# One list of weights for a two-layer trunk, and a freer order of its mixing stage, on one core

## The chip, the core and the metric

The kernel runs on one core of a Trainium2 chip. The core has five engines that run at the same time: TensorE (PE; its loads of the stationary operand are listed apart, as PEld), VectorE (DVE), ScalarE (ACT), GpSimd (POOL) and SyncE (SP), which here only starts transfers (DMA) between DRAM and the on-chip memory. Matmul results land in PSUM banks. Each engine works through its own instructions in order, and waits where an input is not there or a buffer is not free.

The metric is the device time of one launch in microseconds (us), the median over runs.

## The reference

A trunk of two layers on one sequence of 512 tokens with 1024 features, and 256 memory tokens. Each layer applies four steps, each behind an RMSNorm and added to the stream h:

```
h = h + 0.5 * (silu(u @ w_gate) * (u @ w_up)) @ w_out          # ffn1, 2816 wide
p = rmsnorm(h) @ w_mix_in                                       # 3712 columns
h = h + concat(short_conv(p_conv), hgrn2(p_hg), rwkv7(p_rw)) @ w_mix_out
h = h + softmax(q @ k_mem.T / 16) @ v_mem @ wo                  # 4 heads, k and v from rmsnorm(mem)
h = h + 0.5 * ffn2(rmsnorm(h))
```

`hgrn2` is a gated linear recurrence with 6 heads of 64; `rwkv7` is a recurrence with 6 heads of 64 whose state is updated for every token by a decay, a rank-one correction and a rank-one term. After both layers comes a last RMSNorm. All inputs and the output are fp32.

## The kernel before, in words

All activations lie as tiles of 128 features x 512 tokens in 69 slots of on-chip memory (names s_...). h itself is eight such tiles. A product of fp32 operands is made of three matmuls in a rounded format (fp32r): each operand is split into a high and a low part, and w·x, w·x_low and w_low·x are summed in PSUM (`mm3`). A product with 1024 input features is thus 24 matmuls of 128 x 512.

**Weights.** `load_w` fetches one weight tile of 128 x 1024: SP starts the transfer into `wst` (2 buffers), ACT copies it to `whi` in fp32r (3 buffers), DVE subtracts the two into `wlo` (3 buffers). This is "the split" of a weight. In the two feed-forward stages `group` calls `load_w` where the product stands in the program. In the mixing and cross-attention stages the products are in a queue, `Fill`, and `Fill.load` calls `load_w` for the next three products of that queue (AHEAD = 3). The queue of a stage is empty before the stage begins, and the products of the mixing stage's output are added to it only once their inputs are there, so the look-ahead does not pass the border of a stage.

**Order.** PE keeps program order. While the program is written out, a planner (`Clock`) keeps an estimate of when each engine is free and each tile is written; DVE's and ACT's instructions are put in order of their planned start. In the mixing and cross-attention stages `Fill.run` picks, again and again, between the next step (three matmuls) of the queue and the next piece of one of several chains of work, written as generators. A generator says what it needs (`Need`: tiles, finished products, free slots, free PSUM banks); its piece is taken once the planned time of these, less an allowance `ahead`, plus MARGIN (0.4 us) lies before PE's planned time. Generators marked calm are held back while DVE has more than 5 us of planned work.

**The mixing stage** (`mix`) first stores h in DRAM. Its 29 input products run in the order: RWKV decay, three pairs (of heads) of RWKV k, r, v, three pairs of HGRN f, v, q, gate, the RWKV gate, and two blocks of the convolution (cz, cx, cb). Among them run, as generators:

- `rw_inputs`, three times: prepares an RWKV pair;
- `rw_solve`: inverts 96 triangular 32 x 32 systems on DVE, in 30 steps of a multiplication and an addition each (tile G); behind it `rw_chain`, the serial recurrence over the chunks, and `rw_post`;
- one generator for HGRN: the gates of pair 0, then pair 0 with the gates of pair 1 in its middle, then pair 1 with those of pair 2, then pair 2, then the eight products of the stage's output over y columns 5 to 8. It starts when RWKV's third pair is prepared (key in2). Pair 2's four tiles wait in DRAM until they are used;
- `normed`: the norm of the memory tokens for the cross-attention (four tiles: two scalings by `rmem` and a split each). It waits for the convolution product cb0 (key), and in its loop for 8 and 7 free slots.

Then come the keys and values from the memory tokens (16 weight tiles) and the output products over columns 0 to 5.

In the `kernel.py` of before, line L286 stands for every instruction of DVE, ACT, POOL and SP (a wrapper that records them), L341 for every matmul and L345 for every transpose. Instructions are told apart by tile names: pb, pm, pt are PSUM banks (3, 3 and 2 of them), s a slot, vec a table of per-feature constants.

## Time and profile before

| what | value |
|---|---|
| time, median of 3 runs | 2483.07 us (2482.79 to 2483.42) |
| time of the profiled execution | 2484.71 us |
| span in its profile | 2482.9 us |
| granted TensorE clock, mean | 0.985 |
| PE busy | 2410.2 us, 97% |
| DVE busy | 1383.0 us, 56% |
| ACT busy | 997.0 us, 40% |
| mean DMA rate | 98 GB/s |

The span is the profiled stretch of one execution; about 1.8 us lie outside it. "Busy" leaves out waiting. The two layers take about 1230 us each; in the first, ffn1 ends near 380 us, mixing near 760 us, cross-attention near 880 us. A row of the timeline gives start, duration, engine, operation, the tile written and those read, and in brackets the idle time of the engine just before the row and what ended it. A row of the windows gives a stretch of the span, for each engine its busy time and number of instructions, then the granted clock as a share of full speed, the share of the DMA engines in use, and GB/s.

### The profile page before, as it was taken

The page shows a single profiled execution, that of the slowest core. Times are in us where ns is not written, and L with a number is a line of the kernel's source. Part 1 is how long each engine was busy: PE and PEld are TensorE (multiplying, and loading weights), DVE is VectorE, ACT ScalarE, POOL GpSimd, SP SyncE. Part 2 cuts the span into 40 slices and gives each one's busy share as a digit, 9 for nine tenths or more (in the row PEclk, how much of TensorE's full clock was granted, in tenths as well). Part 3 has the DMA queues.
Part 4 walks back from the last instruction along what each step waited for, and adds up shares of the span by engine and source line. Part 5 has one row for each costly group of instructions (what it writes and reads, how often), then busy time and mean ns, then how long its engine had stood idle before and what let it go on. Part 6 is the DMA issues. An engine that isn't in the chain of part 4 may idle for free.

```text
span 2482.9 us, 33542 instructions
## 1 busy us (share of the span) xinstructions
PE 2410.2 (97%) x13812; PEld 1977.9 (80%) x13812; DVE 1383.0 (56%) x2172; ACT 997.0 (40%) x1426; POOL 15.7 (1%) x22
## 2 busy tenths in 40 slices
PE   7999999999999999999999999999999999999997
PEld 6878887787867878888888888877887687888886
DVE  5434456788766544344544444567886656444344
ACT  4323235675654432222332222366765534322233
POOL 0000000000000000000000000000000000000000
PEclk9999999999999999999999999999999999999998
DMA  4323333233422123232333232423243212232322
GB/s 155 96 85 96 98 112 109 75 119 119 130 84 72 64 92 96 94 101 93 95 100 96 95 99 94 136 83 101 100 124 109 83 57 85 86 101 94 102 92 86
DMA packets 92008, 242.61 MB, mean 98 GB/s; under 512 B 21840, under 2 KB 24528, under 8 KB 91856
## 3 DMA queue, kind: packets, MB, share of 16 engines
q1 hardware_dynamic: 88544, 234.36, 29.9%
q10 hardware_dynamic: 3312, 6.12, 0.7%
q8 instruction: 108, 1.77, 0.3%
q14 instruction: 44, 0.36, 0.0%
HBM read 228.39 MB, written 12.06 MB: 97 GB/s over the span
## 4 chain that ended last, share of the span: by engine, by line
PE 89%; DVE 5%; ACT 4%; issue 1%; DMA 0%; SPq 0%; POOLq 0%; DVEq 0%; ACTq 0%
PE pb L341 80%; PE pm L341 6%; DVE s L286 4%; ACT s L286 3%; PE pt L341 1%; ACT L286 1%; PE pm L345 1%; DVE wlo L286 1%; ACT whi L286 0%; PE pt L345 0%; DMA s<-xT 0%; DVE G L286 0%; SPq L286 0%; ACT UV L286 0%; POOLq L1654 0%
## 5 line engine op out<-in xcount | busy, mean ns | idle before, releaser
L341 PE MATMUL pb<-s,whi 128*128 128x512 f32 (+1 forms) x6160 | 1901.1, 391 | 13.8 <-ACT whi L286 10.7
L341 PEld LDWEIGHTS pb<-s,whi 128*128 128x128 f32 x6160 | 1153.6, 190 | 258.0 <-ACT whi L286 12.4
L341 PE MATMUL pb<-s,wlo 128*128 128x512 f32 (+1 forms) x3080 | 1196.1, 388 | 30.0 <-DVE wlo L286 30.0
L341 PEld LDWEIGHTS pb<-s,wlo 128*128 128x128 f32 x3080 | 584.6, 190 | 153.8 <-DVE wlo L286 35.4
L286 ACT ACTIVATE s<-s 128x512 f32<-128x512 f32 (+2 forms) x458 | 284.5, 630 | 836.8 <-DVE s L286 835.0
L286 ACT ACTIVATE whi<-wst 128x1024 fp32r<-128x1024 f32 (+5 forms) x445 | 424.2, 969 | 394.7 <-PE pb L341 135.2
L286 DVE TENSOR_TENSOR wlo<-wst,whi 128x1024 fp32r<-128x1024 f32 (+5 forms) x445 | 495.9, 1116 | 153.2 <-ACT whi L286 152.4
L286 DVE TENSOR_TENSOR s<-pb,s 128x512 f32<-128x512 f32 (+1 forms) x345 | 236.6, 689 | 413.5 <-PE pb L341 363.7
L286 DVE TENSOR_TENSOR s<-s,s 128x512 f32<-128x512 f32 (+3 forms) x526 | 318.0, 622 | 144.2 <-ACT s L286 136.0
L286 DVE SCALAR_TENSOR_TENSOR s<-pb,s 128x512 f32<-128x512 f32 x96 | 66.4, 692 | 237.4 <-PE pb L341 237.4
L286 ACT ACT_TABLE_LOAD x84 | 107.8, 1283 | 3.1 <-PEq L1647 1.7
L286 DVE SCALAR_TENSOR_TENSOR s<-s,vec,s 128x512 fp32r<-128x512 f32 (+2 forms) x100 | 74.6, 750 | 9.4 <-ACT s L286 9.0
L341 PE MATMUL pm<-s,s 64*64 64x64 f32 (+2 forms) x1104 | 67.2, 256 | 10.5 <-DVE s L286 10.5
L341 PEld LDWEIGHTS pm<-s,s 64*64 64x64 f32 (+2 forms) x1104 | 62.5, 166 | 17.3 <-DVE s L286 10.8
L286 ACT ACTIVATE s<-s,vec 128x512 fp32r<-128x512 f32 (+1 forms) x90 | 64.4, 719 | 3.3 <-DMA s<-xT 1.7
L286 ACT COPY s<-pm 64x256 f32<-64x256 f32 (+3 forms) x69 | 23.3, 358 | 76.9 <-PE pm L341 66.0
L341 PE MATMUL pb<-whi,s 128*128 128x512 f32 x128 | 47.2, 414 | 0.0
L341 PEld LDWEIGHTS pm<-s 64*64 64x64 f32 (+1 forms) x1152 | 33.9, 130 | 9.6 <-issue 6.9
L341 PE MATMUL pm<-s 64*64 64x32 f32 (+1 forms) x1152 | 37.7, 216 | 0.0
L286 ACT ACTIVATE s<-pb 128x512 fp32r<-128x512 f32 x32 | 18.8, 596 | 37.0 <-PE pb L341 36.8
L286 DVE TENSOR_TENSOR s<-s 128x256 f32<-128x256 f32 (+1 forms) x79 | 31.4, 436 | 0.1
L341 PEld LDWEIGHTS pb<-whi,s 128*128 128x128 f32 x128 | 24.0, 188 | 6.0
(106 smaller groups left out, 726.5 us busy)
## 6 DMA issues: line engine op xcount, KB each, us to landing
wst<-ffn_w_in SPq DMA_DIRECT2D x175, 512.0 KB, 3.5
wst<-w_mix_in SPq DMA_DIRECT2D x58, 512.0 KB, 3.5
wst<-ffn_w_out SPq DMA_DIRECT2D x64, 448.0 KB, 3.3
wst<-ffn_w_out SPq DMA_DIRECT2D x32, 512.0 KB, 3.5
wst<-xattn_wk SPq DMA_DIRECT2D x16, 512.0 KB, 3.7
wst<-xattn_wv SPq DMA_DIRECT2D x16, 512.0 KB, 3.6
wst<-xattn_wq SPq DMA_DIRECT2D x16, 512.0 KB, 3.5
wst<-xattn_wo SPq DMA_DIRECT2D x32, 256.0 KB, 2.6
```

The source lines that it names most:

```text
L286: ins = fn(*args, **kw)
L341: self.pin(nc.tensor.matmul(*args, **kw))
L345: self.pin(nc.tensor.transpose(*args, **kw))
```

## The change

1. **One list of weights** (`Weights`, object W). The plan of all weight tiles, in the order in which the products run, is written before anything else (`plan_ffn`, `plan_mix`, `plan_xa`). `take` hands out the first entry; before and after each product the next tiles of the list are loaded and split until three are ahead (two while a product is under way), across stages and for products that are not in the queue yet. `Fill.load` goes, and `group` in the feed-forward stages takes from the same list. The buffers stay 2, 3 and 3.
2. **HGRN pairs.** Three generators in place of one, each waiting for its own gate product and 11 slots (7 for pair 0), no longer for RWKV's third pair. The last to end queues the output products. Pair 1's four tiles go through DRAM as pair 2's did: 8 stores and 8 fetches of 256 KB more over both layers.
3. **Memory norm.** `normed` waits for the product hv2 (HGRN, pair 2) and 12 free slots instead of cb0, and for 6 and 5 free slots in place of 8 and 7 in its loop.
4. **Constants.** MARGIN 0.4 to 0.15 us; the allowance `ahead` of a step of `rw_solve` 4.0 to 8.0 us.

The number of matmuls stays. Loads of ACT's function tables in the program go from 84 to 74.

```diff
@@ -104,10 +104,9 @@
 NSLOT = 69
 AHEAD = 3
-MARGIN = 0.4
+MARGIN = 0.15
 CALM = 5.0
 SPARE = 3
-NEXTAT = 2
 INF = 1 << 40
@@ -470,6 +469,31 @@
             ve.tensor_tensor(lo[:, cs], st[:, cs], f32(hi[:, cs]), op=ALU.subtract)
         return hi, lo
+    class Weights:
+        def __init__(self):
+            self.plan = deque()
+        def add(self, src, cols=1024):
+            self.plan.append([src, cols, None])
+        def ahead(self, n):
+            for e in list(self.plan)[:n]:
+                if e[2] is None:
+                    e[2] = load_w(*e[:2])
+        def take(self, src, cols):
+            have, c, w = self.plan[0]
+            assert (have.name, have.offset, c) == (src.name, src.offset, cols)
+            if w is None:
+                self.ahead(1)
+            w = self.plan.popleft()[2]
+            self.ahead(AHEAD - 1)
+            return w
+    W = Weights()
     def mm3(ps, w, wl, x, xl, start, stop):
         te.matmul(ps, w, x, start=start, stop=False)
         te.matmul(ps, w, xl, start=False, stop=False)
@@ -482,9 +506,10 @@
             mm3(ps, w[0][:, k * P:(k + 1) * P], w[1][:, k * P:(k + 1) * P], xh, xl, k == 0, k == n - 1)
             yield
-    def group(ps, src, cols, xs, w=None):
-        for _ in group_steps(ps, w or load_w(src, cols), xs):
+    def group(ps, src, cols, xs):
+        for _ in group_steps(ps, W.take(src, cols), xs):
             pass
+        W.ahead(AHEAD)
     class Fill:
...
@@ -508,33 +533,27 @@
                 return group_steps(box[0], w, xs)
             self.add(key, src, cols, steps, lambda: post(box[0]), room=room, xs=xs)
-        def load(self, n):
-            for e in list(self.q)[:n]:
-                if e[5] is None and e[1] is not None:
-                    e[5] = load_w(e[1], e[2])
-
         def ready(self):
             if self.cur:
                 return clock.pe
             if not self.q:
                 return None
-            e = self.q[0]
-            if (e[6] and e[6] not in self.done) or len(sl.free) < e[7]:
+            after, room, xs = self.q[0][5:]
+            if (after and after not in self.done) or len(sl.free) < room:
                 return None
-            self.load(AHEAD)
-            return max([bigs.free_at()] + [clock.when(x) for x in e[5] or ()]
-                       + [clock.when(x) for y in e[8][:3] for x in y])
+            W.ahead(AHEAD)
+            return max([bigs.free_at()] + [clock.when(x) for y in [W.plan[0][2]] + list(xs[:3]) for x in y])
         def step(self):
             if self.cur is None:
-                self.load(AHEAD)
-                key, _, _, steps, post, w = self.q.popleft()[:6]
-                self.cur = (key, iter(steps(w) or ()), post)
+                key, src, cols, steps, post = self.q.popleft()[:5]
+                self.cur = (key, iter(steps(W.take(src, cols)) or ()), post)
             key, g, post = self.cur
             if next(g, self) is self:
                 self.cur = None
                 self.done.add(key)
+                W.ahead(AHEAD)
                 if post:
                     post()
...
@@ -706,7 +725,7 @@
                 if f in between:
                     between[f]()
                 pg = big()
-                group(pg, w_in[l, f], 1024, n.x, between.get("w") if f == 0 else None)
+                group(pg, w_in[l, f], 1024, n.x)
                 if f or "w" not in between:
                     n.begin()
                 pu = small() if first else big()
@@ -974,7 +993,7 @@
             ve.tensor_tensor(tv, Gv[:, 0:k, k:k + 1].to_broadcast([n, k, w]),
                              Bv[k // 16][:, k % 16:k % 16 + 1, k + 1:].to_broadcast([n, k, w]), op=ALU.mult)
             ve.tensor_tensor(Gv[:, 0:k, k + 1:], Gv[:, 0:k, k + 1:], tv, op=ALU.add)
-            yield Need(Gv[:, 0:k, k + 1:], ahead=4.0)
+            yield Need(Gv[:, 0:k, k + 1:], ahead=8.0)
         sl.put(tmp, *B)
         sp.dma_start(Td, G[0:n, :])
         F.done.add((l, "solved"))
@@ -1125,7 +1144,7 @@
         sl.put(gd)
     def hg_gates(l, st, p):
-        q, f, v, g = (fetch(f"{w}{p}") if p == 2 else st["X"][f"{w}{p}"] for w in ("hq", "hf", "hv", "hgate"))
+        q, f, v, g = (fetch(f"{w}{p}") if p else st["X"][f"{w}{p}"] for w in ("hq", "hf", "hv", "hgate"))
         lb = lbt[:, l, p:p + 1]
         x, m, e1, e2 = sl.get(), sl.get(), sl.get(), sl.get()
@@ -1164,19 +1183,9 @@
         se.activation(dec, b3[:, :, C - 1], AF.Exp)
         return q, k, v, g, b, kh, dec
-    def hg_pairs(l, st, ys):
-        gates = []
-
-        def gate(p):
-            yield Need(keys=[(l, f"hg{p}"), (l, "in2")], room=11 if p == 2 else 7)
-            gates.append((yield from hg_gates(l, st, p)))
-
-        yield from gate(0)
-        for p in range(3):
-            yield from hg_pair(l, p, gates[p], ys, gate)
-
-    def hg_pair(l, p, gates, ys, gate):
-        q, k, v, g, b, kh, dec = gates
+    def hg_pair(l, st, p, ys):
+        yield Need(keys=[(l, f"hg{p}")], room=11 if p else 7)
+        q, k, v, g, b, kh, dec = yield from hg_gates(l, st, p)
         def tok(x):
...
@@ -1325,7 +1332,7 @@
                 X[key] = evac(n, ps)
                 if fn:
                     fn(X[key])
-                if key in ("hq2", "hf2", "hv2", "hgate2"):
+                if key[0] == "h" and key[-1] != "0":
                     send(key, X[key])
             add(key, j, post)
...
@@ -1372,15 +1380,16 @@
                     nxt.chunk(d)
             F.product((l, f"o{c0}{d}"), a["w_mix_out"][l, d, :, c0 * P:c1 * P], (c1 - c0) * P, ys, post)
-        def hgrn():
-            yield from hg_pairs(l, st, yb)
-            for d in range(ND):
-                yield Need(room=3)
-                unpark(d)
-                out(d, 5, 8, yb)
+        def hgrn(p):
+            yield from hg_pair(l, st, p, yb)
+            if all(yb):
+                for d in range(ND):
+                    yield Need(room=3)
+                    unpark(d)
+                    out(d, 5, 8, yb)
         F.run(seq(rw_solve(l, st), rw_chain(l, st), rw_post(l, st, ya)), mem_normed(),
-              calm=[rw_inputs(l, n, st, p) for p in range(3)] + [hgrn()])
+              calm=[rw_inputs(l, n, st, p) for p in range(3)] + [hgrn(p) for p in range(3)])
         ya += yc
         for d in range(ND):
             out(d, 0, 5, ya, True)
@@ -1422,11 +1431,11 @@
         mn, mx = [], []
         def normed():
-            yield Need(keys=[(l, "cb0")])
+            yield Need(keys=[(l, "hv2")], room=12)
             for i in range(4):
-                yield Need(room=8)
+                yield Need(room=6)
                 m = load_mem(i)
-                yield Need(m, room=7)
+                yield Need(m, room=5)
                 for u in range(2):
                     x = m[:, u * MEM:(u + 1) * MEM]
                     ve.scalar_tensor_tensor(x, x, col(l, "mem_norm", 2 * i + u), rmem, op0=ALU.mult, op1=ALU.mult)
@@ -1575,13 +1584,47 @@
         return nxt
+    def plan_ffn(l, which):
+        w_in, w_out = a[f"ffn{which}_w_in"], a[f"ffn{which}_w_out"]
+        for f0, f1 in SLABS:
+            for f in range(f0, f1):
+                W.add(w_in[l, f])
+                W.add(w_in[l, NF + f])
+            for d in range(ND):
+                W.add(w_out[l, d, :, f0 * P:f1 * P], (f1 - f0) * P)
+    def plan_mix(l):
+        rw, hg = ([[b + i + p for i in o] for p in range(3)] for b, o in ((RW0, (3, 0, 6)), (HG0, (3, 6, 0, 9))))
+        order = [RW0 + 9] + rw[0] + rw[1] + rw[2] + hg[0] + hg[1] + hg[2] + [RW0 + 10]
+        for j in order + [i + j for i in range(2) for j in (2, 4, 0)]:
+            W.add(a["w_mix_in"][l, j])
+        for j in range(2 * XH):
+            W.add(a["xattn_wk"][l, j])
+        for e in range(2):
+            for kp in range(4):
+                W.add(a["xattn_wv"][l, e, kp])
+        for c0, c1 in ((5, 8), (0, 5)):
+            for d in range(ND):
+                W.add(a["w_mix_out"][l, d, :, c0 * P:c1 * P], (c1 - c0) * P)
+    def plan_xa(l):
+        for d in range(ND):
+            W.add(a["xattn_wq"][l, d])
+        for h0 in range(2):
+            for d in range(ND):
+                W.add(a["xattn_wo"][l, d, :, 4 * h0 * P:4 * (h0 + 1) * P], 4 * P)
     steps = [(l, s) for l in range(L) for s in ("ffn1", "mix", "xa", "ffn2") if s in parts]
     norms = {"ffn1": "ffn1_norm", "mix": "mix_norm", "xa": "xattn_norm", "ffn2": "ffn2_norm"}
-    n, first_w = start("ffn1_norm", a["ffn1_w_in"][0, 0])
+    plans = {"ffn1": lambda l: plan_ffn(l, 1), "mix": plan_mix, "xa": plan_xa, "ffn2": lambda l: plan_ffn(l, 2)}
+    for l, s in steps:
+        plans[s](l)
+    n = start("ffn1_norm", a["ffn1_w_in"][0, 0])
     for i, (l, s) in enumerate(steps):
         nxt = Norm(steps[i + 1][0], norms[steps[i + 1][1]]) if i + 1 < len(steps) else Norm(None, None)
         if s == "ffn1":
-            n = ffn(l, 1, n, nxt, {"w": first_w, 9: mem_sums, 11: mem_rms, 12: mem_spread} if l == 0 else {})
+            n = ffn(l, 1, n, nxt, {"w": True, 9: mem_sums, 11: mem_rms, 12: mem_spread} if l == 0 else {})
         elif s == "mix":
             n, kv = mix(l, n, nxt)
         elif s == "xa":
```

Three places show what moves; line L285 stands in the changed kernel where L286 stood. The first is DVE at the end of the first layer's mixing stage, where the last output products are added to h (s<-pb,s), the next norm's sum of squares is kept (the rows with one name twice), and the input of the cross-attention is split (SCALAR_TENSOR_TENSOR). Before:

```order
L286 SCALAR_TENSOR_TENSOR s_408_6376<-s_371_5965,vec,s_407_6375 128x512
L286 TENSOR_TENSOR s_372_5967<-pb,s_372_5967 128x512
L286 TENSOR_TENSOR s_391_6223<-s_391_6223,s_409_6396 128x512
L286 SCALAR_TENSOR_TENSOR s_411_6400<-s_372_5967,vec,s_410_6399 128x512
L286 TENSOR_TENSOR s_373_5969<-pb,s_373_5969 128x512
L286 TENSOR_TENSOR s_391_6223<-s_391_6223,s_412_6420 128x512
L286 SCALAR_TENSOR_TENSOR s_414_6424<-s_373_5969,vec,s_413_6423 128x512
L286 TENSOR_TENSOR wlo<-wst,whi 128x1024 x3
```

and in the change:

```order
L285 TENSOR_TENSOR s_372_5901<-pb,s_372_5901 128x512
L285 TENSOR_TENSOR wlo<-wst,whi 128x1024
L285 TENSOR_TENSOR s_395_6245<-s_395_6245,s_413_6424 128x512
L285 SCALAR_TENSOR_TENSOR s_415_6428<-s_372_5901,vec,s_414_6427 128x512
L285 TENSOR_TENSOR s_373_5903<-pb,s_373_5903 128x512
L285 TENSOR_TENSOR wlo<-wst,whi 128x1024
L285 TENSOR_TENSOR s_395_6245<-s_395_6245,s_416_6454 128x512
L285 SCALAR_TENSOR_TENSOR s_418_6458<-s_373_5903,vec,s_417_6457 128x512
```

Before, the first three weight splits of the cross-attention stood together behind the last split of an input; in the change they stand among the evacuations of the last output products. The border from cross-attention to ffn2 and the start of the stage's output products move alike.

The second is DVE in the middle of the mixing stage: the memory norm (rows with rmem) and the solve (rows with G). Before:

```order
L286 SCALAR_TENSOR_TENSOR s_282_4431<-s_282_4431,vec,rmem 128x256 x2
L286 TENSOR_TENSOR s_283_4435<-pb,s_283_4435 128x512
L286 TENSOR_TENSOR s_285_4459<-s_282_4431,s_284_4458 128x512
L286 TENSOR_TENSOR s_287_4479<-s_283_4435,s_286_4478 128x512
L286 SCALAR_TENSOR_TENSOR s_288_4482<-s_288_4482,vec,rmem 128x256 x2
L286 COPY_PREDICATED s_248_3807<-cst,pm 128x256
```

and in the change:

```order
L285 TENSOR_TENSOR G<-G,s_250_3807 96x21x10
L285 TENSOR_TENSOR wlo<-wst,whi 128x1024
L285 TENSOR_TENSOR s_253_3943<-pb,s_151_2722 128x512
L285 SCALAR_TENSOR_TENSOR s_254_3947<-s_254_3947,vec,rmem 128x256 x2
L285 SCALAR_TENSOR_TENSOR s_257_3955<-s_257_3955,vec,rmem 128x256 x2
L285 TENSOR_TENSOR s_256_3952<-s_254_3947,s_255_3951 128x512
L285 TENSOR_TENSOR s_259_3960<-s_257_3955,s_258_3959 128x512
L285 SCALAR_TENSOR_TENSOR s_260_3963<-s_260_3963,vec,rmem 128x256 x2
L285 SCALAR_TENSOR_TENSOR s_263_3971<-s_263_3971,vec,rmem 128x256 x2
```

Before, the memory norm ran after the solve, the last of it ahead of a merge of HGRN scores (COPY_PREDICATED, which empties a pm bank); in the change its four tiles stand in one piece inside the solve.

The third is DVE at the first RWKV pair, where `rw_shift` mixes a product with its neighbour token (SCALAR_TENSOR_TENSOR of 128x511). Before:

```order
L286 TENSOR_TENSOR s_167_2846<-s_155_2735,s_160_2792 64x4x64
L286 SCALAR_TENSOR_TENSOR s_169_2853<-s_168_2851,vec,s_169_2853 128x511
L286 TENSOR_TENSOR wlo<-wst,whi 128x1024
L286 TENSOR_TENSOR s_170_2887<-pb,s_151_2716 128x512
```

and in the change:

```order
L285 TENSOR_TENSOR s_167_2846<-s_155_2741,s_160_2795 64x4x64
L285 TENSOR_TENSOR wlo<-wst,whi 128x1024
L285 SCALAR_TENSOR_TENSOR s_169_2859<-s_168_2857,vec,s_169_2859 128x511
L285 TENSOR_TENSOR wlo<-wst,whi 128x1024
```

The split of a weight now stands ahead of that row instead of behind it.

More of the change, by code (lines that the diff above doesn't have):

```diff
@@ L497, in add @@
         def add(self, key, src, cols, steps, post=None, after=None, room=2, xs=()):
-            self.q.append([key, src, cols, steps, post, None, after, room, xs])
+            self.q.append((key, src, cols, steps, post, after, room, xs))
         def product(self, key, src, cols, xs, post, room=2):
@@ L680, in load @@
                 n.x.append(split(h[d], col(0, name, d)))
-        w = load_w(src, 1024, 256, load)
+        W.plan[0][2] = load_w(src, 1024, 256, load)
         n.name = None
@@ L685, in start @@
             n.chunk(d)
-        return n, w
+        return n
     def ffn(l, which, n, nxt, between=None):
@@ L1260, in hg_pair @@
                 sl.put(q, b)
-            if i == NEXTAT and p < 2:
-                yield from gate(p + 1)
         yield Need(att, S, qh, banks=[(smalls, 1)])
@@ L1351, in mix @@
             add_rw(f"v{p}", 6 + p)
-        add_hg(0)
+            if p == 2:
+                add_hg(0)
         add_hg(1)
```

## The prediction

> **What bounds the kernel now.** I read the page first, then PE's waits by what ended them, then PE's timeline at the large waits, then windows behind each of them.
>
> ```profile
> span 2482.9 us, 33542 instructions
> PE 2410.2 (97%) x13812; PEld 1977.9 (80%) x13812; DVE 1383.0 (56%) x2172; ACT 997.0 (40%) x1426; POOL 15.7 (1%) x22
> ```
>
> PE is busy for 2410.2 of 2482.9 us, and the change leaves every matmul in place. All that can be won is PE's idle time, 72.7 us, and the stretches in which it runs at a lower clock. Of the idle time the start (before 43 us) and the final norm are not touched. The waits, as releaser, us, times and largest:
>
> ```profile
> PE pb L341 <- DVE wlo L286: 30.0, 12, 3.6
> ```
>
> That is PE waiting for the split of a weight. The largest of these waits, and two for DVE to empty a bank of HGRN scores (pm), lie here in PE's timeline:
>
> ```profile
> 168.25 0.50 PE L341 MATMUL pb<-s,wlo 128*128 128x512 f32 x1 [3.58 <-DVE wlo L286]
> 428.29 0.50 PE L341 MATMUL pb<-s,wlo 128*128 128x512 f32 x1 [2.86 <-DVE wlo L286]
> 597.27 1.01 PE L341 MATMUL pm<-s,s 64*64 64x64 f32 x13 [5.27 <-DVE s L286]
> 727.55 0.73 PE L341 MATMUL pb<-s,whi 128*128 128x512 f32 x2 [0.39 <-ACT whi L286]
> 730.38 0.50 PE L341 MATMUL pb<-s,wlo 128*128 128x512 f32 x1 [2.09 <-DVE wlo L286]
> 761.40 0.80 PE L341 MATMUL pb<-s,wlo 128*128 128x512 f32 x1 [3.53 <-DVE wlo L286]
> 882.81 0.56 PE L341 MATMUL pb<-s,wlo 128*128 128x512 f32 x1 [3.53 <-DVE wlo L286]
> 1949.94 0.51 PE L341 MATMUL pb<-s,wlo 128*128 128x512 f32 x1 [2.10 <-DVE wlo L286]
> 1982.61 0.80 PE L341 MATMUL pb<-s,wlo 128*128 128x512 f32 x1 [3.53 <-DVE wlo L286]
> 2102.75 0.80 PE L341 MATMUL pb<-s,wlo 128*128 128x512 f32 x1 [3.53 <-DVE wlo L286]
> 1646.61 0.50 PE L341 MATMUL pb<-s,wlo 128*128 128x512 f32 x1 [2.86 <-DVE wlo L286]
> 1815.61 0.69 PE L341 MATMUL pm<-s,s 64*64 64x64 f32 x7 [5.27 <-DVE s L286]
> ```
>
> The second layer repeats the first. 727 to 731, 761 and 883 us are the places where one queue of products ends and the next begins: the stage's output, the border to cross-attention, the border to ffn2. The idle time is not the whole price, for the clock behind it is low (stretch, busy times, then clock, DMA share and GB/s):
>
> ```profile
> 168.25:173.10 4.85, 4.84 (x14) 3.86 (x15) 1.09 (x1) 0.00 (x0) 0.00 (x0) 0.65 0.59 218
> 428.29:432.50 4.21, 4.21 (x16) 3.25 (x17) 4.02 (x6) 3.01 (x6) 0.00 (x0) 0.60 0.39 125
> 597.27:603.20 5.93, 5.92 (x71) 5.81 (x72) 4.46 (x8) 1.75 (x3) 0.00 (x0) 0.50 0.72 204
> 730.38:734.00 3.62, 3.62 (x16) 3.00 (x17) 1.62 (x3) 0.71 (x1) 0.00 (x0) 1.00 0.59 180
> 761.40:767.05 5.65, 5.65 (x13) 4.46 (x14) 1.97 (x2) 1.06 (x1) 0.00 (x0) 0.50 0.57 187
> 882.81:886.50 3.69, 3.69 (x9) 2.93 (x10) 1.08 (x1) 0.14 (x1) 0.00 (x0) 0.54 0.61 193
> 1646.61:1651.10 4.49, 4.49 (x17) 3.46 (x18) 4.29 (x6) 3.29 (x6) 0.00 (x0) 0.62 0.42 122
> 1815.61:1821.80 6.19, 6.19 (x73) 6.07 (x74) 4.18 (x8) 1.86 (x3) 0.00 (x0) 0.50 0.68 199
> 1949.94:1955.00 5.06, 5.06 (x15) 4.03 (x16) 1.65 (x3) 0.74 (x1) 0.00 (x0) 0.66 0.43 133
> 1982.61:1986.00 3.39, 3.39 (x9) 2.73 (x10) 1.08 (x1) 0.00 (x0) 0.00 (x0) 0.56 0.62 185
> 2102.75:2108.50 5.75, 5.75 (x14) 4.49 (x15) 1.08 (x1) 1.06 (x1) 0.00 (x0) 0.50 0.57 182
> ```
>
> A stretch of t us at clock c loses t x (1 - c). A wait of 2.09 us kept the clock (1.00), one of 2.10 us lost it (0.66), and so did all of 2.86 us and more.
>
> **The change part by part.**
>
> *Hand-overs of the queue.* Why does PE wait 3.53 us at 761 us? DVE there:
>
> ```profile
> 759.46 0.75 DVE L286 SCALAR_TENSOR_TENSOR s<-s,vec,s 128x512 fp32r<-128x512 f32 x1
> 760.13 2.35 DVE L286 TENSOR_TENSOR wlo<-wst,whi 128x1024 fp32r<-128x1024 f32 x2
> ```
>
> The weight's split stands behind the last work of the stage before, although its tile was free long ago; SP and ACT had brought it earlier. In the change it stands several evacuations further ahead (first excerpt of the order), so that PE finds it done. The gaps are 0.39 + 2.09 and about 0.39 + 2.10 at the output products, and 4 x 3.53 at the borders: 19.1 us. The low clock behind them cost 5.65 x 0.50 = 2.8, 3.39 x 0.44 = 1.5, 3.69 x 0.46 = 1.7, 5.75 x 0.50 = 2.9 and 5.06 x 0.34 = 1.7, together 10.6 us. The sum is 29.7 us. The border to ffn2 is the tight one: its products before are half as long (12 matmuls), and DVE has a split, an evacuation, a sum and a normed split to do in each. I leave 1.0 us of each of these two gaps: **-27.7 us**. Bounds: -29.7, and nothing if the three buffers cannot hold the next stage's weights.
>
> *ffn1, 168 us.* The split stands behind work of the block before, of which
>
> ```profile
> 166.38 0.69 DVE L286 TENSOR_TENSOR s<-s,s 128x512 fp32r<-128x512 f32 x1 [0.69 <-ACT s L286]
> ```
>
> is the last. In the change it goes ahead of a multiplication and this subtraction, that is from the end of this row, 167.0 us, to about 165.3 us, 1.7 us sooner; with 1.9 us of wait left the clock holds, as it did at 730 us, and 4.85 x 0.35 = 1.7 us come with it: **-3.4 us** (bounds -1.7 and -5.3).
>
> *First RWKV pair, 428 us.* The split moves ahead of one scaling:
>
> ```profile
> 426.35 0.75 DVE L286 SCALAR_TENSOR_TENSOR s<-s,vec,s 128x511 f32<-128x511 f32 x1
> ```
>
> 0.67 us sooner, which leaves 2.2 us, near the 2.09 and 2.10 us of which one lost the clock and one did not. I take half of the clock's 4.21 x 0.40 = 1.7 us: 1.5 us a layer, **-3.0 us** (bounds 0 and -9.1, the whole of both gaps and clocks).
>
> *Memory norm, 597 us.* PE waits 5.27 us for a merge of HGRN scores, and DVE does this ahead of it:
>
> ```profile
> 592.87 0.87 DVE L286 SCALAR_TENSOR_TENSOR s<-s,vec,rmem 128x256 f32<-128x256 f32 x2
> ...
> 596.50 0.72 DVE L286 COPY_PREDICATED s<-cst,pm 128x256 f32<-128x256 int32 x1
> ```
>
> The rmem scalings and their subtractions take 592.87 to 596.50 us less one evacuation, 3.0 us. They move away (second excerpt). That leaves 2.3 us of wait and, again by half, 5.93 x 0.50 / 2 = 1.5 us of clock: 4.5 us a layer, **-9.0 us** (bounds 0 and -16.6).
>
> *What is late instead.* The memory norm and the solve meet in the change, and the solve may run 8 instead of 4 us ahead. DVE's load in this stretch, a stretch of ffn1 for the time of a matmul, and the additions of the solve (shortest, median and longest in ns):
>
> ```profile
> 510.00:550.00 40.00, 40.00 (x318) 32.41 (x317) 34.01 (x81) 28.43 (x41) 0.16 (x1) 1.00 0.31 102
> 550.00:600.00 50.00, 44.73 (x317) 37.07 (x316) 47.98 (x90) 27.68 (x34) 1.59 (x3) 0.96 0.42 125
> 250.00:300.00 50.00, 50.00 (x223) 41.40 (x222) 20.67 (x24) 11.32 (x13) 0.00 (x0) 1.00 0.28 92
> L286 DVE TENSOR_TENSOR G<-G,s x60: 185/346/406, 517.1 to 1803.8; 96x30 f32<-96x30 f32 x4, 96x58 f32<-96x58 f32 x4, 96x84 f32<-96x84 f32 x4, 96x108 f32<-96x108 f32 x4
> ```
>
> DVE is busy for 82.0 of 90 us and gets no more to do; only the order decides. In the change 26 rows of the solve stand between two weight splits at one place (13 steps, at the 0.39 us of the larger forms 10 us), and at another all four memory tiles with solve steps between them. A product takes 24 matmuls, 5.4 us by 223 of them in 50 us, and three weights ahead are 16 us of cover; 10 us of solve with the evacuations, shifts and HGRN gates that come due at the same time use it up. The wait that follows has no row; the nearest is the 2.86-us wait behind a split with its 1.7 us of clock. I take it once a layer: 2 x 4.5 = **+9.0 us**. Bounds: -7.0 for both layers (no new wait, and HGRN work let loose earlier fills the small waits of the serial RWKV chain, 15.00 - 11.51 = 3.5 us a layer by the row below), and +16.5 (a wait like that at 597 us with its clock, 5.27 + 3.0).
>
> ```profile
> 689.00:704.00 15.00, 11.51 (x218) 8.86 (x214) 9.52 (x23) 8.93 (x16) 0.00 (x0) 1.00 0.11 33
> ```
>
> *Pair 1 through DRAM* adds 16 transfers on SP's queue, between weight loads. Pair 2's four fetches already stand there:
>
> ```profile
> 600.78 0.33 SPq L286 DMA_DIRECT2D s<-hq  x1
> ...
> 604.58 0.33 SPq L286 DMA_DIRECT2D wst<-xattn_wk  x1
> ```
>
> They hold the next weight back by 3.8 us, less than one product. I cost them at nothing; the cover is the weights ahead. Without it each weight held back costs its transfer and split (fifth rival). MARGIN and the fewer function-table loads on ACT, busy 40%, I also cost at nothing: the loads' work lies beside PE.
>
> Sum: 27.7 + 3.4 + 3.0 + 9.0 - 9.0 = 34.1. From the profiled execution's 2484.7 us this gives 2450.6; that execution stands 1.6 us above the median, so **2449 us**.
>
> [...]
>
> **The rivals.**
>
> 1. *The forecast*, 2449 us, own range 2436 to 2462.
> 2. *The mixing stage keeps its merge wait and gets another.* The hand-overs, ffn1 and the first pair gain 34.1, the memory norm's 9.0 is lost to solve steps standing in its place, and each layer has one new wait of 8.2 us (5.27 + 3.0) in place of 4.5: 2484.7 - 34.1 + 16.4 - 1.6 = **2465 us**. For it: DVE at 47.98 of 50 us. Against: the pieces that moved are 3.0 us of the 5.27.
> 3. *All of it goes.* 29.7 + 5.3 + 9.1 + 16.6 + 7.0 = 67.7 us: **2415 us**. Against: DVE's load in mixing leaves little room to have everything on time.
> 4. *The list does not reach over the borders*, because two wst and three wlo buffers hold the next weight until the stage before has read its own. Then only ffn1 and mixing change, -3.4 - 3.0 - 9.0 + 9.0: **2477 us**. Against: the order of DVE shows the splits ahead of the last evacuations.
> 5. *Slower: SP's queue blocks.* A fetch of pair 1 or 2 needs a free slot; if the slot's last reader is late, every weight load behind the fetch waits. By the transfers (KB each, us to landing)
>
> ```profile
> wst<-w_mix_in SPq DMA_DIRECT2D x58, 512.0 KB, 3.5
> ```
>
> a weight so held costs a transfer of 3.5 us, a split on ACT and DVE of about 1.2 us each (2.35 for two above) and 1.7 us of clock, about 7.5 us. From five such weights over both layers it eats the 34.1; with three a layer, 2484.7 - 34.1 + 45.0 - 1.6 = **2494 us**. For it: eight more fetches in the busiest stretch. Against: the rows at 600 us, where four pass without a wait of PE.
>
> **How the numbers follow.** Chances: the forecast 0.50, rival two 0.22, three 0.12, four 0.07, five 0.09. A difference from no change can be told from 0.2%, 5 us: faster is below 2478, slower above 2488. The first three are faster throughout, and half of the fourth: 0.86 with the second's tail taken off. Same: 0.06, from the fourth and the fifth's near side. Slower: 0.08. For eight times in ten the range needs the forecast, most of the second and fourth, and the upper half of the third: 2420 to 2476.
>
> **What would show it.** Right: no wait over 1.5 us at the six hand-overs, and clock 1.00 behind them; about 1.9 us left near 168; a merge wait of 2 to 3 us in place of 5.27; one new wait for wlo between 500 and 600 us and its repeat in the second layer. PE's busy time should fall by some 12 us, its idle time by some 20. Wrong: gaps of 3.5 us still at 761 and 883 us (rival four); waits for whi behind a fetch of HGRN tiles on SP (five); or a mixing stage longer than before, which would mean that the order on DVE, not the weights, was the larger matter.

## The result, and the profile after

The changed kernel takes **2447.7 us** (median of 4 runs, 2439.96 to 2447.92) against 2482.9 us before on the same chips: ratio 0.985, 95% interval 0.983 to 0.987. The forecast was 2449. Its profiled execution took 2447.83 us with a span of 2446.0 us, 36.9 us less than before. The page of the changed kernel:

```profile
span 2446.0 us, 33922 instructions
PE 2398.0 (98%) x13812; PEld 1971.5 (81%) x13812; DVE 1389.6 (57%) x2172; ACT 995.7 (41%) x1416; POOL 20.8 (1%) x22
```

and PE's waits (releaser: us, times, largest), the four largest groups:

```profile
PE pb L340 <- ACT whi L285: 16.7, 4, 7.7
PE pb L340 <- DVE s L285: 9.8, 7, 2.2
PE pb L340 <- DVE wlo L285: 5.6, 5, 1.8
PE pm L340 <- DVE s L285: 3.1, 5, 2.2
```

The waits for wlo went from 30.0 to 5.6 us, those of HGRN and norm matmuls (pm) for DVE from 12.7 to 3.1. The waits for whi went up, from 10.7 to 16.7, and those of products for a DVE tile from 1.9 to 9.8. PE is idle 24.7 us less and busy 12.2 us less; the latter is the clock (mean 0.985 before, 0.990 after), since the matmuls are the same 13812. Windows of the changed kernel show the places that were costed (columns as before; PE's busy time, then the clock after the five engines):

```profile
165.00:170.00 5.00, 5.00 (x24) 4.15 (x23) 3.02 (x6) 1.26 (x3) 0.00 (x0) 1.00 0.34 105
421.49:425.00 3.51, 3.51 (x19) 2.82 (x20) 3.32 (x5) 1.49 (x3) 0.00 (x0) 1.00 0.66 165
604.80:610.00 5.20, 4.45 (x21) 3.74 (x22) 4.29 (x6) 4.94 (x8) 0.00 (x0) 0.67 0.31 101
689.00:704.00 15.00, 15.00 (x65) 10.11 (x64) 7.10 (x12) 10.42 (x16) 0.00 (x0) 1.00 0.12 36
714.86:719.00 4.14, 4.14 (x11) 3.28 (x12) 2.61 (x4) 0.74 (x1) 0.00 (x0) 0.59 0.58 158
740.00:750.00 10.00, 10.00 (x50) 8.41 (x48) 6.95 (x9) 5.14 (x7) 0.00 (x0) 1.00 0.48 159
866.05:872.00 5.95, 5.67 (x22) 4.44 (x23) 2.41 (x6) 1.06 (x1) 1.91 (x1) 0.74 0.33 109
1807.53:1815.00 7.47, 6.97 (x31) 6.12 (x31) 4.99 (x7) 7.18 (x10) 0.00 (x0) 0.54 0.21 73
1864.03:1869.10 5.07, 5.07 (x92) 4.66 (x94) 3.08 (x6) 1.34 (x4) 0.00 (x0) 0.66 0.55 185
1919.80:1924.00 4.20, 4.20 (x12) 3.33 (x13) 2.61 (x4) 0.74 (x1) 0.00 (x0) 0.59 0.54 156
2071.00:2077.30 6.30, 6.01 (x22) 4.76 (x23) 2.42 (x6) 1.06 (x1) 1.91 (x1) 0.73 0.38 128
```

The border to cross-attention, now at 744 us, lies in a stretch with PE busy for 10.00 of 10.00 us at full clock: that wait of 3.53 us is gone, and so is the wait in ffn1. At 605, 715 and 866 us the clock is low (0.67, 0.59 and 0.74): new waits stand there. In PE's timeline:

```profile
421.49 0.50 PE L340 MATMUL pb<-s,wlo 128*128 128x512 f32 x1 [1.27 <-DVE wlo L285]
604.80 0.51 PE L340 MATMUL pb<-s,whi 128*128 128x256 f32 x2 [3.34 <-ACT whi L285]
606.06 0.57 PE L340 MATMUL pb<-s,wlo 128*128 128x256 f32 x1 [0.75 <-DVE wlo L285]
660.35 0.50 PE L340 MATMUL pb<-whi,s 128*128 128x512 f32 x1 [1.64 <-DVE s L285]
714.86 0.78 PE L340 MATMUL pb<-s,whi 128*128 128x512 f32 x2 [2.18 <-DVE s L285]
866.05 0.50 PE L340 MATMUL pb<-s,whi 128*128 128x512 f32 x1 [0.50 <-ACT s L285]
```

### The profile page after: what moved, and what is told of

Same layout as the page of the kernel before. It is cut to its first block, busy times and chain, and to the rows that moved or that the text cites. A ratio compares the mean times of both kernels' runs of the same rounds, so it can differ in the third digit from the quotient of the medians.

```text
span 2446.0 us, 33922 instructions
## 1 busy us (share of the span) xinstructions
PE 2398.0 (98%) x13812; PEld 1971.5 (81%) x13812; DVE 1389.6 (57%) x2172; ACT 995.7 (41%) x1416; POOL 20.8 (1%) x22
## 3 DMA queue, kind: packets, MB, share of 16 engines
q8 instruction: 109, 1.79, 0.3%
## 5 line engine op out<-in xcount | busy, mean ns | idle before, releaser
L340 PE MATMUL pb<-s,whi 128*128 128x512 f32 (+1 forms) x6160 | 1897.6, 390 | 24.3 <-ACT whi L285 16.7
L285 ACT ACTIVATE whi<-wst 128x1024 fp32r<-128x1024 f32 (+5 forms) x445 | 434.2, 976 | 1033.9 <-PE pb L340 637.6
L285 DVE TENSOR_TENSOR wlo<-wst,whi 128x1024 fp32r<-128x1024 f32 (+5 forms) x445 | 498.4, 1121 | 134.8 <-ACT whi L285 127.1
L285 DVE TENSOR_TENSOR s<-pb,s 128x512 f32<-128x512 f32 (+1 forms) x345 | 236.0, 689 | 465.0 <-PE pb L340 443.4
L285 ACT ACTIVATE s<-s 128x512 f32<-128x512 f32 (+2 forms) x458 | 282.7, 626 | 246.8 <-DVE s L285 241.2
L285 DVE TENSOR_TENSOR s<-s,s 128x512 f32<-128x512 f32 (+3 forms) x526 | 317.0, 621 | 97.0 <-ACT s L285 92.1
L285 DVE SCALAR_TENSOR_TENSOR s<-pb,s 128x512 f32<-128x512 f32 x96 | 66.4, 692 | 234.5 <-PE pb L340 234.5
L285 DVE SCALAR_TENSOR_TENSOR s<-s,vec,s 128x512 fp32r<-128x512 f32 (+2 forms) x100 | 74.3, 748 | 3.8 <-ACT s L285 2.9
L285 ACT ACTIVATE s<-s,vec 128x512 fp32r<-128x512 f32 (+1 forms) x90 | 64.3, 718 | 3.3 <-DMA s<-xT 1.7
L285 POOL TENSOR_TENSOR rms<-rms,mhalf 128x4 f32<-128x4 f32 (+1 forms) x10 | 17.1, 1714 | 2120.7 <-DVE rms L285 2120.7
L285 DVE TENSOR_TENSOR s<-s 128x256 f32<-128x256 f32 (+1 forms) x79 | 31.7, 439 | 0.2
L285 ACT ACTIVATE s<-pb 128x512 fp32r<-128x512 f32 x32 | 19.0, 594 | 29.5 <-PE pb L340 29.2
```

The costliest lines, as they stand in the source:

```text
L285: ins = fn(*args, **kw)
L340: self.pin(nc.tensor.matmul(*args, **kw))
```

## The experiments

Each was timed in three rounds beside the kernel before, whose medians in these comparisons were 2482.3 to 2483.6 us. Five runs take one part out of the changed kernel, two add a single part to the kernel before, and five follow what these showed. Three of the latter (e8, e9, e11) do more than take parts in or out and stand below only.

| kernel | list | pairs at once | norm sooner | solve 8.0 | MARGIN 0.15 | us | ratio, 95% interval |
|---|---|---|---|---|---|---|---|
| before | - | - | - | - | - | 2482.9 | 1 |
| e1 | yes | - | - | - | - | 2470.5 | 0.995 (0.993 to 0.996) |
| e10 | - | yes | - | - | - | 2496.5 | 1.005 (1.004 to 1.007) |
| e12 | yes | - | yes | - | - | 2504.2 | 1.008 (1.007 to 1.010) |
| e5 | - | - | yes | yes | yes | 2510.1 | 1.011 (1.010 to 1.013) |
| e2 | - | yes | yes | yes | yes | 2460.5 | 0.991 (0.990 to 0.993) |
| e3 | yes | - | yes | yes | yes | 2486.1 | 1.002 (1.001 to 1.003) |
| e4 | yes | yes | - | yes | yes | 2452.6 | 0.988 (0.987 to 0.990) |
| e6 | yes | yes | yes | - | yes | 2465.2 | 0.993 (0.991 to 0.994) |
| e7 | yes | yes | yes | yes | - | 2480.0 | 0.999 (0.998 to 1.000) |
| the change | yes | yes | yes | yes | yes | 2447.7 | 0.985 (0.983 to 0.987) |

Taken out one at a time the five parts are worth 12.8, 38.4, 4.9, 17.5 and 32.3 us: 106 us, three times the 35 us that they bring together. Added to the kernel before, the list brings 12 us, the pairs lose 13, and the list with the norm loses 21; MARGIN and the solve's allowance were not added alone. The prices do not add up, so each holds only beside the other parts.

**e1, the list alone.** The kernel before with the list of weights and nothing else:

```diff
+    W = Weights()
...
+        for _ in group_steps(ps, W.take(src, cols), xs):
             pass
+        W.ahead(AHEAD)
```

> The kernel before with the list of weights alone; pairs, memory norm, MARGIN and the solve's allowance as before. Theory (the list and the rest add up): the six hand-overs (19.1 us idle and 10.6 us of clock before, 1.6 and 3.4 left in the changed kernel) and the wait at 168 us (3.6 and 1.7) go: 2482.9 - 24.7 - 5.3 = about 2453 us. The waits at 428 us (2.86) and at the merge (5.27) and their repeats stay. Rival (the parts need each other): the look-ahead shifts the splits of the mixing stage too and opens waits there that the freer pairs had closed; then the time is above 2460 us with waits for wlo or whi between 430 and 700 us.

2470.5 us: the rival's time, but not its form, since no wait for a weight above 0.84 us opens between 430 and 700 us. The border waits go, but the merge wait grows. PE's timeline, the stretch in which it starves and the memory norm's scalings (count, shortest, median and longest in ns, first and last start) of e1:

```profile
592.26 0.50 PE L341 MATMUL pm<-s 64*64 64x32 f32 x5 [9.65 <-DVE s L286]
581.49:600.00 18.51, 8.31 (x113) 8.06 (x113) 18.33 (x42) 6.68 (x11) 0.00 (x0) 0.63 0.23 72
L286 DVE SCALAR_TENSOR_TENSOR s<-s,vec,rmem x8: 456/479/480, 585.0 to 597.5; 128x256 f32<-128x256 f32 x8
```

From 581.5 to 596.6 us PE runs no product: the input products are used up, the key products need the memory norm, whose last scaling starts at 597.5, and PE has only pieces of HGRN while DVE does the norm, the solve and splits for 18.33 of 18.51 us. Much of what the list wins at the borders it loses here, by letting the products run out.

**e12, the list and the norm sooner.** e1 with the norm's wait as in the change:

```diff
-            yield Need(keys=[(l, "cb0")])
+            yield Need(keys=[(l, "hv2")], room=12)
...
```

> The kernel before with the list and the memory norm sooner; pairs in a row, MARGIN 0.4, solve 4.0 as before. Theory (in e1 the list uses up the input products by 581 us, the norm ends at 597 us, and PE has only HGRN pieces in between, 9.65 us idle and 6.8 of clock): with the norm sooner these 16 us a layer go, and the last HGRN pair runs bare at the end as in e3, where 13 us of waits and 14 of clock stood between 687 and 723 us: so the loss moves, 2460 to 2490 us, with no wait over 3 us before 640 us and waits of PE for DVE near 690 to 720 us. Rival (the list's own weight splits crowd out the scores): the wait near 592 us stays.

2504.2 us, outside the expected times, with the expected form. Norm and windows of e12:

```profile
L286 DVE SCALAR_TENSOR_TENSOR s<-s,vec,rmem x8: 472/476/478, 528.6 to 534.2; 128x256 f32<-128x256 f32 x8
581.00:600.00 19.00, 17.84 (x248) 17.13 (x248) 17.16 (x32) 8.71 (x12) 1.05 (x2) 1.00 0.54 156
684.00:735.00 51.00, 40.71 (x476) 28.77 (x476) 29.90 (x66) 29.96 (x51) 0.00 (x0) 0.74 0.15 52
```

The starved stretch is nearly full and at full clock; 10.3 us of idle and a clock of 0.74 stand at the end of the stage, and 7.4 us with a clock of 0.84 just before, between 640 and 684 us. The products only move forward and are missing later, where the last pair and the RWKV chain run bare.

**e3, pairs in a row again, and e5, that without the list.** The changed kernel with one generator for the three pairs; e5 also loads weights as before:

```diff
-              calm=[rw_inputs(l, n, st, p) for p in range(3)] + [hgrn(p) for p in range(3)])
+              calm=[rw_inputs(l, n, st, p) for p in range(3)] + [hgrn()])
```

> The changed kernel with one generator for the HGRN pairs again, pair 1 not through DRAM. Theory: the new waits at 605 and 1808 us (ACT busy with the gates of two pairs and their function tables: 4.1 + 1.7 and 3.8 + 3.4 us with the clock) go, the small waits of the RWKV chain's end come back (3.5 us a layer and 1.7 us of clock once): 2447.7 - 13.0 + 8.7 = about 2443 us. Rival: the pairs at the same time are what took the merge wait of 5.27 us away; then it is back with its clock, +16.6, and the time is about 2460 us.

> The changed kernel with neither the list nor the pairs at the same time; memory norm sooner, MARGIN 0.15 and the solve's allowance 8 stay. Theory (with the pairs in a row the last pair runs bare at the end of the mixing stage, list or no list): hand-overs and the tail both cost, 2486 + 12.8 (what the list brings beside free pairs) = about 2499 us, with PE waits for DVE's scores near 690 to 720 us. Rival (it is the list that uses up the products too soon): without it the tail is covered again, 2480 us or less.

2486.1 and 2510.1 us. Both theories for e3 fell. The first had the right waits go, but the end of the stage costs far more than the small waits of before. The rival's merge wait is not back either: from 575 to 617 us PE is busy for 42.00 of 42.00 us at full clock. New is a wait of 5.30 us at the value products, at 654 us. The end of the stage in e3 and in the changed kernel, e3 first:

```profile
684.00:726.00 42.00, 26.95 (x348) 22.04 (x348) 23.06 (x54) 20.59 (x36) 0.00 (x0) 0.65 0.08 22
```

```profile
684.00:726.00 42.00, 39.82 (x189) 28.70 (x188) 26.70 (x44) 23.01 (x37) 0.00 (x0) 0.96 0.28 84
```

With the pairs in a row PE works 27 of 42 us at a clock of 0.65, in 348 matmuls, nearly all of them small ones of the last pair, with no input, key or value products between them. e5 agrees: list or not, the tail is there (from 684 to 735 us PE works 35.65 of 51 us at a clock of 0.70), though the time is 11 us above the theory's.

**e10, the pairs at once alone**, on the kernel before (the same edit the other way round):

> The kernel before with the HGRN pairs at the same time alone (no list, norm waits for cb0, MARGIN 0.4, solve 4.0). Theory (the parts of the mixing stage work only together: pairs started sooner take pieces' place and slots while the norm, and with it the next products, come late): no gain, 2480 to 2500 us. Rival (the pairs alone carry what the rest brings without the list): about 2460 us.

2496.5 us, as the theory has it: no gain. Its largest new wait is 5.37 us at 734.81 us, PE waiting on ACT for an input of the last output products. The solve with its old allowance ends late there, at 600 us. One thing e10 does bring: the merge wait of 5.27 us is gone, although the norm's last scaling still starts at 599 us. In its place PE waits 2.85 us at 600 us, for the input of a key product.

**e2, the changed kernel without the list:**

> The changed kernel without the list: weights loaded as before, all else changed. Theory (parts add up): what the list does not bring, 35.2 - 30.0 = 5 us, is left: about 2478 us; waits of 3.53 us at the two borders and about 2.1 us at the output products are there in both layers, the merge wait of 5.27 us is not. Rival: without the list the mixing stage's new work has less cover and the time is at 2483 us or above.

2460.5 us; both theories missed. The border waits are back, one of them here with the two that stand in place of the 4.1 us at 605 us:

```profile
609.31 0.50 PE L340 MATMUL pb<-s,whi 128*128 128x256 f32 x2 [0.71 <-ACT whi L285]
610.57 0.39 PE L340 MATMUL pb<-s,wlo 128*128 128x256 f32 x1 [0.76 <-DVE wlo L285]
...
750.32 0.50 PE L340 MATMUL pb<-s,wlo 128*128 128x512 f32 x1 [3.53 <-DVE wlo L285]
```

The waits of 3.58 us in ffn1 and of 2.85 us at the first RWKV pair are back as well. Inside the mixing stage, however, e2 waits less: 1.5 us at 609, nothing above 0.25 at the value products and 1.4 at 719 us, where the changed kernel has 4.1, 1.6 and 2.2. Between the two the list is worth 12.8 us net.

**e4, the norm late again:** the edit of e12 taken back in the changed kernel.

> The changed kernel with the memory norm waiting for cb0 and 8 and 7 slots again. Theory of the prediction: the norm's 3.0 us stand ahead of a merge again and PE waits there, 4.5 to 8.2 us a layer with the clock: 2457 to 2464 us. Rival: the freer pairs moved the merge itself, the norm's place does not matter: 2446 to 2450 us.

2452.6 us, between the two. The merge wait of 5.27 us does not come back. The edit does not bring back the norm's old time either: its scalings run from 576.2 to 580.4 us, where they ended at 601 us before, and they are just in time. A wait of 5.28 us for a DVE tile stands at the value products, at 664 us, and one of 3.03 us at 705 us; the wait at 605 us is down to 0.68 us.

**e6, the solve's allowance at 4.0:**

```diff
-            yield Need(Gv[:, 0:k, k + 1:], ahead=8.0)
+            yield Need(Gv[:, 0:k, k + 1:], ahead=4.0)
```

> The changed kernel with the solve's allowance at 4.0 us as before. Theory of the prediction (26 rows of the solve between two splits make PE wait): some 4.5 us a layer are won, about 2439 us. Rival by the trace of the changed kernel, which has no wait of PE for DVE between 516 and 600 us: nothing is won there; the solve ends later and with it the serial chain behind it, and the end of the mixing stage gets waits: 2450 to 2465 us.

2465.2 us, the rival. The solve's last steps, in e6 and in the changed kernel:

```profile
L285 DVE TENSOR_TENSOR G<-G,s x30: 178/348/405, 509.9 to 580.1; 96x30 f32<-96x30 f32 x2, 96x58 f32<-96x58 f32 x2, 96x84 f32<-96x84 f32 x2, 96x108 f32<-96x108 f32 x2
721.66 0.80 PE L340 MATMUL pb<-s,whi 128*128 128x512 f32 x1 [5.07 <-ACT s L285]
```

```profile
L285 DVE TENSOR_TENSOR G<-G,s x30: 178/346/403, 512.6 to 550.6; 96x30 f32<-96x30 f32 x2, 96x58 f32<-96x58 f32 x2, 96x84 f32<-96x84 f32 x2, 96x108 f32<-96x108 f32 x2
```

The same operations end at 580 instead of 551 us, and the work that follows them in series comes late: PE waits 5.07 us for the input of the last output products, and 3.75 us at the value products (655 us), where the changed kernel waits 2.18 and 1.64 us.

**e7, MARGIN at 0.4, and e9, that with the norm ahead of the pairs:**

```diff
-MARGIN = 0.15
+MARGIN = 0.4
...
-        yield Need(keys=[(l, f"hg{p}")], room=11 if p else 7)
+        yield Need(keys=[(l, f"hg{p}")] + ([(l, "xm")] if p else []), room=11 if p else 7)
```

> The changed kernel with MARGIN at 0.4 us as before. Theory of the prediction: no effect beyond 0.2%, 2443 to 2453 us. Rival: 0.25 us at each of some hundred pieces lets products go first where a piece of the chain was due; the products are used up sooner and the last pieces run bare at the end of the mixing stage: above 2460 us.

> As e7_margin04 (the changed kernel with MARGIN 0.4), but HGRN pairs 1 and 2 wait until the memory norm is done. Theory (in e7 the pairs take the slots, the norm ends only at 604 us, and from 576 us on PE has no product ready): the norm ends before the input products do, the waits between 575 and 605 us and the low clock behind them (17.1 us a layer) go: 2455 us or less. Rival (with the larger margin the products are used up too soon whatever the norm does): waits of the same size later in the stage, 2470 us or more.

e7 takes 2480.0 us: 0.25 us in a planner's rule is worth nearly the whole change. The norm, two waits of PE and a window of e7, then the same window of the changed kernel:

```profile
L285 DVE SCALAR_TENSOR_TENSOR s<-s,vec,rmem x8: 474/477/485, 529.1 to 603.8; 128x256 f32<-128x256 f32 x8
586.88 1.97 PE L340 MATMUL pm<-s,s 64*64 64x64 f32 x32 [5.52 <-ACT s L285]
596.25 2.77 PE L340 MATMUL pt<-s,s 32*32 32x32 f32 x96 [7.39 <-DVE s L285]
575.00:617.00 42.00, 22.41 (x410) 20.86 (x409) 28.95 (x63) 22.79 (x40) 0.00 (x0) 0.59 0.21 60
```

```profile
575.00:617.00 42.00, 37.91 (x572) 33.68 (x572) 33.19 (x59) 35.15 (x53) 0.00 (x0) 0.96 0.30 94
```

The norm starts at 529 and is only done at 603.8 us, so that no product is ready. The stretch costs 19.6 us of idle time and 22.4 x 0.41 = 9.2 us of clock, and the second layer has the same waits (4.91 and 7.39 us); the changed kernel loses 5.6 us in this window. So the rival's time came true, but not its place: the end of the stage, 684 to 735 us, is full in e7 (50.99 of 51 us). Made to wait for the norm, the pairs let it end at 539 us, and e9's window reads

```profile
575.00:617.00 42.00, 39.23 (x622) 36.33 (x621) 35.94 (x67) 26.61 (x38) 0.00 (x0) 1.00 0.50 157
```

The waits at that place are gone, as the theory has it, but the time is 2471.7 us, as the rival has it, and not 2455: others came later, one of 5.99 us at 645.65 us. So the order of norm and pairs is the cause of e7's starved stretch, and that stretch is where e7 loses its time. With it filled, three quarters of the loss, 24 us, come back at later places; why the larger margin opens waits there stays open.

**e8, pair 2 behind pair 1's gates, and e11, that with the allowance at 12.0:**

```diff
-        yield Need(keys=[(l, f"hg{p}")], room=11 if p else 7)
+        yield Need(keys=[(l, f"hg{p}")] + ([(l, "gates1")] if p == 2 else []), room=11 if p else 7)
...
+        F.done.add((l, f"gates{p}"))
```

> The changed kernel where HGRN pair 2 also waits until pair 1's gates are done. Theory (the wait at 605 us comes from the gates of two pairs on ACT at once, six function-table loads of 1.28 us between 589 and 607 us ahead of a weight's copy): that wait goes in both layers, 3.34 + 0.75 + 1.7 and 3.34 + 0.5 + 3.4 us: about 2435 us. Rival: pair 2 is now late and PE waits for it at the end of the stage: 2448 us or more.

> As e8_stagger (pair 2 waits for pair 1's gates), with the solve's allowance at 12 us. If a sooner end of the solve and of the serial chain behind it is what the allowance brings (from 4 to 8 us it was worth 17 us), a little more may come, at the wait before the last output products (1.9 us and 1.7 of clock a layer): 2431 to 2438 us. If DVE's order is used up at 8 us, 2438 to 2450 us.

2438.1 us (ratio 0.982, 0.980 to 0.983) and **2433.5 us** (0.980, 0.978 to 0.982): both beat the changed kernel, e11 by 14 us. What ACT does in the changed kernel ahead of the weight's copy for which PE waits at 604.80:

```profile
592.58 1.28 ACT L285 ACT_TABLE_LOAD   x1
...
595.67 1.28 ACT L285 ACT_TABLE_LOAD   x1
...
598.66 1.28 ACT L285 ACT_TABLE_LOAD   x1
599.95 1.16 ACT L285 ACTIVATE s<-s 128x512 f32<-128x512 f32 x2
601.12 1.28 ACT L285 ACT_TABLE_LOAD   x1
602.42 0.63 ACT L285 ACTIVATE s<-s 128x512 f32<-128x512 f32 x1
603.08 0.72 ACT L285 ACTIVATE s<-s,oml 128x512 f32<-128x512 f32 x1
603.71 1.04 ACT L285 ACTIVATE whi<-wst 128x1024 fp32r<-128x1024 f32 x1
```

Two pairs' gates alternate there; with one more load at 589.59 us, five loads of 1.28 us stand ahead of the copy, not six as expected above. Staggered, the wait in e8 is

```profile
612.78 0.50 PE L340 MATMUL pb<-s,whi 128*128 128x256 f32 x2 [0.94 <-ACT whi L285]
```

0.94 in place of 3.34 us, in both layers. PE is idle 4.5 us less than in the changed kernel, all of it at this place; the rest of the 9.8 us between the two spans is clock (mean 0.990 there, 0.993 in e8), in part behind waits that the edit leaves in place (866, 1864 and 1919 us). So the overlap is what makes this wait long in the changed kernel, but the overlap alone is not enough: e2, e4 and e6, whose pairs are as free, have no single wait above 0.76, 0.68 and 1.24 us at the key products. It seems that a weight's copy has also to come due within the overlap, which no run isolated. How much of it is the table loads and how much the gates' other work was not separated. e11's last gain is within what single runs of these kernels differ (2433.3 to 2437.4 against 2434.0 to 2439.1). With e11's allowance of 12 us PE does wait among the rows of the solve, 0.74 us at 527 us and, behind the four memory tiles, 1.79 us:

```profile
545.41 0.47 PE L340 MATMUL pb<-s,whi 128*128 128x512 f32 x1 [1.79 <-DVE s L285]
```

## Why the prediction was right or wrong

The total was right, 34.1 us forecast and 36.9 found between the spans, but that it is so close is luck: the errors of the terms cancel. Both layers, from the windows and timeline rows above; a wait plus its stretch times (1 - clock):

| term | forecast | found | from |
|---|---|---|---|
| hand-overs | -27.7 | -24.9 | 29.7 less 2 x 0.8 idle and 5.95 x 0.26 + 6.30 x 0.27 of clock |
| ffn1 | -3.4 | -5.3 | no wait, clock 1.00 |
| first RWKV pair | -3.0 | -6.6 | 2.86 to 1.27 us, clock 1.00 |
| merge wait | -9.0 | -16.6 | no wait left |
| chain's small waits | 0 | -8.4 | 15.00 of 15.00 us busy; 3.5 before, and 3.2 + 1.7 of clock in layer 2 |
| new waits | +9.0 | +25.6 | 5.8 + 1.6 + 3.9 at 605, 660, 715; 7.3 + 3.4 + 3.6 in layer 2 |

The found terms make 36.2 of the 36.9 us. Four of them brought 21.5 us more than forecast, and the other two took 19.4 us of it back. The second layer's chain before, for the fifth of them:

```profile
1907.00:1922.00 15.00, 11.76 (x223) 9.68 (x220) 8.32 (x21) 8.67 (x15) 0.00 (x0) 0.89 0.12 39
```

*Hand-overs:* right, in place, size and mechanism. e2 brings the 3.53 us back, e1 takes them away without any other part (no wait above 0.8 us at its borders). Rival four, buffers that hold the list back, is out. The clock behind the border to ffn2 was costed at nothing and cost 1.6 us a layer, against the sign named beforehand, a clock of 1.00 there.

*ffn1 and first pair:* right in mechanism. The waits shrank by more than the rows moved: the term is a third too small in ffn1, where 1.9 us were to be left and nothing is, and half too small at the pair, 3.0 for 6.6 us.

*Merge wait:* the step that failed is "They move away (second excerpt). That leaves 2.3 us of wait". I took the wait for a queue on DVE that gets 3.0 us shorter. It was also a lack of products: PE had nothing but that merge to go on with, because the key products behind it needed the norm. Before, the last input product ended at 591 us and the first key product started at 600.73 us. e1 made the lack worse (9.65 us), e12 with its earlier norm filled it, and so did e10 with free pairs alone. In the changed kernel the norm ends at 538 us instead of 601:

```profile
L285 DVE SCALAR_TENSOR_TENSOR s<-s,vec,rmem x8: 470/476/483, 533.8 to 538.0; 128x256 f32<-128x256 f32 x8
```

The whole wait went, and its clock. Rival two, which kept this wait, is out.

*The chain's small waits* stood only in a bound, by HGRN work let loose earlier. That is what the runs show: no wait above 0.25 us of the chain's matmuls (pt) stands at the end of the stage in e2, e4, e6, e7 and e10, whose pairs are free, while e1, with the pairs in a row, has them. The mechanism was named, its 8.4 us were left out of the sum.

*New waits:* one a layer and its cause were named, "26 rows of the solve stand between two weight splits". Wrong: no wait of PE stands in the solve's stretch, 512 to 551 us, and e6, which takes the burst away, is slower by 17.5 us. Waits among the solve's rows do stand in e11 with the larger allowance (1.79 us), but also in e6 with the smaller one (1.19 us for a split, at 555 us). The new waits are on ACT's gates of two pairs (605 us, e8), at the value products (660) and at the last output products (715): three a layer, and nearly three times the price. What brings those at 660 and 715 us into being was not isolated.

*MARGIN and the pairs* had no term of their own: "MARGIN and the fewer function-table loads on ACT, busy 40%, I also cost at nothing". e7 prices MARGIN at 32.3 us within this set. The pairs entered only through a bound of 3.5 us a layer; e3 prices them at 38.4. Taken-out prices do not add up, so these are no terms that the sum could have held. They show what it did not hold: the mixing stage is a fixed store of products beside a long serial chain, and its time hangs on whether a product is ready whenever the chain waits. e1, e3, e7 and e12 show the same starved stretch at different places; that this one account covers every wait of the stage is argued, not shown.

*SP's queue* (rival five) did not block: the fetches of pairs 1 and 2 pass between 570 and 595 us, and the one weight that came late there was held by ACT and DVE (waits of 3.34 us for whi and 0.75 us for wlo at 605 us). *The third rival*, all the listed gains at once, is not reached by e11 either, at 2433.5 against 2415.

*The clock behind a wait.* The prediction let it hold with 1.9 us of wait left at 168 us, as it did behind the 2.09 us at 730 us, and took half of its loss with 2.2 and 2.3 us left. No such length shows in the changed kernel: the clock held behind 1.64 us (1.00 at 660 us) and fell behind 1.63 us (0.66 at 1864 us) and 2.18 us (0.59 at 715 us).

## What to carry to other kernels

Where products are the filler beside a serial chain, do not price an edit by the wait that it touches: ask first how long the filler lasts against the chain, and what each edit does to either end. A look-ahead that wins at stage borders can lose much of it inside a stage by letting the filler run out sooner (in e1 the border waits of 3.53 us went, the merge wait grew from 5.27 to 9.65 us, and 12 us were left). Parts tuned as a set are to be taken out one at a time as well as added one at a time; here the five taken out make 106 us, and of the two added alone one gains about what the other loses.

## What the runs showed of the hardware

At 866 us the clock fell after waits much shorter than its low stretch: two waits of 0.50 and 0.28 us, with eight narrow norm matmuls behind them, were followed by 3.40 us at clock 0.50. In the second layer waits of 0.49 and 0.29 us were followed by 3.30 us at 0.51 (from 2074.00 us). The place at 866 us in e8, again with a wait of 0.50 us, kept it, as did the wait of 1.64 us at 660 us, whose repeat of 1.63 us in the second layer lost it (0.66 above). The three windows, the first two of the changed kernel:

```profile
660.35:665.50 5.15, 5.15 (x143) 4.70 (x145) 3.85 (x9) 2.24 (x6) 0.00 (x0) 1.00 0.66 201
868.90:872.30 3.40, 3.40 (x10) 2.65 (x9) 1.17 (x3) 0.00 (x0) 1.70 (x1) 0.50 0.39 113
```

```profile
862.00:870.00 8.00, 7.45 (x36) 6.10 (x37) 2.66 (x6) 1.27 (x3) 1.90 (x1) 1.00 0.34 112
```

One and the same order of work thus has several times: three of the changed kernel's runs took 2447.6 to 2447.9 us at a mean clock of 0.990, the fourth 2439.96 at 0.994. What decides whether a wait of such a length costs the clock stays open; no run here moved a wait by itself.
